# SSD's group norm taken out of its scan and applied in a pass beside the GLA scan

## The chip, the cores and the metric

The kernel runs on one core of a Trainium2 chip. The metric is the device time in microseconds of one execution of the whole program. A core has a matrix engine (TensorE, PE in the profile, with its weight loads as PEld), a vector engine (VectorE, DVE), a scalar engine (ScalarE, ACT), GpSimd (POOL) and a queue for transfers (SyncE, SP). Each engine works through its own list of instructions in order; semaphores make it wait for others. SBUF is the on-chip memory, PSUM the small memory of eight banks into which PE writes; POOL does not touch PSUM in this kernel.

## The reference

One decoder block on x (1024 tokens x 1024 channels, fp32): norm, one wide projection, two sequence mixers side by side (SSD, a Mamba-2 scan; GLA, gated linear attention), a gated merge, cross-attention to 256 memory tokens, a SwiGLU FFN and a last norm. The change concerns the end of the SSD mixer:

```python
def ssd_mixer(z, xBC, dt_raw, conv_w, conv_b, dt_bias, A_log, D_skip, norm_g):
    ...
    Lmat = segsum_exp(a)
    CB = jnp.einsum('bclgn,bcsgn->bcgls', Cc, Bc)
    y_diag = jnp.einsum('bcgls,bgrcls,bcsgrp->bclgrp', CB, Lmat, X)
    ...
    y_off = jnp.einsum('bclgn,bcgrpn,bgrcl->bclgrp', Cc, prev, jnp.exp(a_cs))
    y = (y_diag + y_off).reshape(Bsz, S, SSD_HEADS, P) + D_skip.astype(jnp.float32)[:, None] * x_heads
    y = y.reshape(Bsz, S, SSD_D_INNER) * jax.nn.silu(z.astype(jnp.float32))
    y = rmsnorm(y.reshape(Bsz, S, G, SSD_D_INNER // G), norm_g.reshape(G, SSD_D_INNER // G))
    return y.reshape(Bsz, S, SSD_D_INNER).astype(z.dtype)
```

So y is gated by silu(z), and then, for each token and each of two groups of 512 channels, divided by the root of the mean of its squares (plus EPS = 1e-6) and multiplied by a weight for each channel. The mixer's result is then multiplied by w_up_ssd.

## The kernel before, in words

**Layout and stages.** Activations lie transposed, 128 channels on the partitions and tokens along the row. The big products (w_in, the merge, the FFN) are split in fp32r halves: a weight block goes through ACT (whi, the rounded part, L224) and DVE (wlo, the rest), into a ring of three buffers each (wring, L227), and each block of a product takes three matmuls (high by high, high by low, low by high). Each 256-column unit of w_in runs as seven such products, named B11, T2, T1, B21, T3, B22 and T4 (class Unit, L276), which PE accumulates in banks acc; the sums of weight blocks that these need (sa, raw) are made on POOL or DVE, whichever two running meters (class Meter, `either`) put earlier. A unit's weights (raw, 1 MB) are loaded one unit ahead (L290), and results go to DRAM through SP (L469).

**What sets the order.** The framework records the instructions in program order with priorities and places each engine's list by its own model of time. `run(main, (side, rate), prio=PRIO)` (L439) takes one step of a generator beside every 1/rate steps of the main one and gives it a higher priority. Scans run in this way beside units of w_in.

**SSD's scan** (class SSD, L864) runs beside the units for r, q, k and one of gs, in 16 steps: 8 chunks of 128 tokens by 2 groups. `load` fetches x (xz, first half), B and C (bc), a broadcast row block (csb) and silu(z) (xz, second half) through SP. `lay` makes CB on PE into one PSUM bank, B's transpose into the same bank (copied out as bt by ACT, L893), and multiplies CB by the mask triu on DVE into the SBUF tile cbm. `decay` makes the decay e on ACT, and DVE multiplies e (128x1024) by cbm. `scan` makes y (bank py) and the new state. `gate` adds D times x (four DVE instructions), multiplies by silu(z) on POOL (128x512) and makes the sum of squares (sq on ACT, two sums on DVE, rd). `stat` sums over partitions with a small PE product (ones by rd) and forms rs by DVE and a POOL power. `norm` spreads rs along the row: DVE scales the identity by rs into diag, PE multiplies ones by diag (`spread`, L215), DVE multiplies y by the bank, and SP stores y to ys_d (L949). The calls are interleaved by `ssd_steps` (L951): scan, then stat of the step before with lay of the next, then gate, then norm of the step before with decay of the next. All small products take one of four PSUM banks called bank.

**GLA's scan** (class GLA, L997) runs beside three units of gs and three of gg in 43 steps over 8 chunks (`gla_steps`, L1074; run at L1108). Its tiles lie in a pool gl of their own.

**After it**, the last gg unit runs, and beside it `fetch` (L1203) loads ys_d block by block (128x1024) and splits it into high and low halves for the product by w_up_ssd; here it also applies ssd_norm, as a scale on ACT and as a scalar operand on DVE. All elementwise helpers record L73, all matmuls L51 and transposes L55, so a row of the profile is told apart by its tiles.

Of the kernel before, what the change touches and what calls it, by code (L numbers as in the profile page):

```python
# [78 lines left out]
def block_kernel(ctx: ExitStack, tc: tile.TileContext, t: dict, out: bass.AP):  # L79
# [39 lines left out]
    vm_d = dram("vm_d", MEM, D)  # L119
    cs_d = dram("cs_d", P, P)  # L120

    def acc():
# [37 lines left out]
    for a in range(2):  # L160
# [8 lines left out]
                       channel_multiplier=-1)  # L169
    mhalf = cp.tile([P, 8], F32, name="mhalf")  # L170
    POOL.memset(mhalf, -0.5)
# [550 lines left out]
    ebl = ep.tile([P, 4, NCH], F32, name="ebl")  # L722
    ewl = ep.tile([P, 4, NCH], F32, name="ewl")

    def conv(u, unit):
# [138 lines left out]
    class SSD:  # L864
# [8 lines left out]
        def load(s):  # L873
            g, tk = s.g, s.tk
            s.L = sp_.tile([P, 8, CH], F32, name="xz", tag="xz", bufs=3)
            SP.dma_start(s.L[:, 0:4], xbc_d[g * 512:(g + 1) * 512, tk].rearrange("(k p) s -> p k s", p=P))
            s.BC = sp_.tile([P, 2, CH], F32, name="bc", tag="bc", bufs=2)
            for i in range(2):
                r0 = 1024 + i * 256 + g * P
                SP.dma_start(s.BC[:, i], xbc_d[r0:r0 + P, tk])  # L880
            s.csb = sp_.tile([P, GH, CH], F32, name="csb", tag="csb", bufs=2)
            SP.dma_start(s.csb.rearrange("p h s -> p (h s)"),
                         cs_d[s.i0:s.i0 + GH, :].rearrange("h s -> (h s)").partition_broadcast(P))
            SP.dma_start(s.L[:, 4:8], sz_d[g * 512:(g + 1) * 512, tk].rearrange("(k p) s -> p k s", p=P))

        def lay(s):
            p = bank()
            PE.matmul(p[:, :P], s.BC[:, 0], s.BC[:, 1], start=True, stop=True)
            PE.transpose(p[:, P:2 * P], s.BC[:, 0], ident)
            s.cbm = sp_.tile([P, CH], F32, name="cbm", tag="cbm", bufs=2)  # L890
            mul(DVE, s.cbm, p[:, :P], triu)
            s.bt = sp_.tile([P, P], F32, name="bt", tag="bt", bufs=2)
            ACT.activation(s.bt, p[:, P:2 * P], AF.Copy)  # L893
            p = bank()
            for k in range(4):
                PE.transpose(p[:, k * P:(k + 1) * P], s.L[:, k], ident)
            s.xd = sp_.tile([P, GH, 64], F32, name="xd", tag="xd", bufs=2)
            mul(DVE, s.xd, p.rearrange("p (h d) -> p h d", d=64), s.heads(dt_h, 64))

        def decay(s):  # L900
            s.e = sp_.tile([P, GH, CH], F32, name="e", tag="e", bufs=2)
            for h in range(GH):
                ACT.activation(s.e[:, h], s.csb[:, h], AF.Relu, bias=cs[:, s.i0 + h:s.i0 + h + 1], scale=-1.0)
            ACT.activation(s.e, s.e, AF.Exp, scale=-1.0)
            ACT.activation(s.csb, s.csb, AF.Exp)
            s.xc = sp_.tile([P, GH, 64], F32, name="xc", tag="xc", bufs=1)
            mul(POOL, s.xc, s.xd, s.heads(dec, 64))
            mul(DVE, s.csb, s.csb, s.BC[:, 1].unsqueeze(1).to_broadcast([P, GH, CH]))
            mul(DVE, s.e, s.e, s.cbm.unsqueeze(1).to_broadcast([P, GH, CH]))

# [16 lines left out]
        def gate(s):  # L927
            s.y = sp_.tile([P, 4, CH], F32, name="y", tag="y", bufs=3)
            for k in range(4):
                DVE.scalar_tensor_tensor(s.y[:, k], s.L[:, k], dcol[:, s.g * 4 + k:s.g * 4 + k + 1],  # L930
                                         s.py[:, k * P:(k + 1) * P], ALU.mult, ALU.add)
            mul(POOL, s.y, s.y, s.L[:, 4:8])
            sq = sp_.tile([P, 4, CH], F32, name="sq", tag="sq", bufs=1)
# [5 lines left out]
        def stat(s):  # L939
            p = bank()  # L940
            PE.matmul(p[:, :1], s.rd, ones[:, :1], start=True, stop=True)
            s.rs = sp_.tile([P, 1], F32, name="rs", tag="rs", bufs=2)
            rsqrt(s.rs, p[:, :1], 1.0 / 512)

        def norm(s):
            p = bank()
            spread(p, s.rs, 1)
            mul(DVE, s.y, s.y, p[:, :P].unsqueeze(1).to_broadcast([P, 4, CH]))
            SP.dma_start(ys_d[s.g * 512:(s.g + 1) * 512, s.tk].rearrange("(k p) s -> p k s", p=P), s.y)  # L949

    def ssd_steps():  # L951
# [7 lines left out]
        for i in range(len(it) + 1):  # L959
# [15 lines left out]
            yield  # L975
            if z:
                z.norm()
            if b:
# [127 lines left out]

    gla = gla_steps()
    run(singles(gs[1:] + gg[:3], B, gg[3:]), (gla, 8 * 5 / 36), prio=PRIO)  # L1108
    drain(gla)
    st4.close()  # L1110
    st_early.close()
# [90 lines left out]

    def fetch(src, dst, gain=None):  # L1203

        for k in range(NB):
            x = hl(dst, k)
            raw = x[:, 1].bitcast(F32)
            SP.dma_start(raw, src[k * P:(k + 1) * P, :])
            if gain:
                ACT.activation(x[:, 0], raw, AF.Copy, scale=col(gain, k))  # L1210
                DVE.scalar_tensor_tensor(x[:, 1], raw, col(gain, k), x[:, 0], ALU.mult, ALU.subtract)
            else:
                ACT.activation(x[:, 0], raw, AF.Copy)
                sub(DVE, x[:, 1], raw, x[:, 0])
            yield
# [13 lines left out]

    get_ys = fetch(ys_d, i_ys, "ssd_norm")  # L1230
    for n, _ in enumerate(group(gg[3:], B)):
# [452 lines left out]
```

## Time and profile before

| What | Value |
|---|---|
| median of 3 runs | 1980.92 us (1979.81 to 1985.29) |
| the profiled execution | 1982.29 us |
| its span, first to last instruction | 1980.6 us |
| granted TensorE clock | 0.995 |
| mean transfer rate | 156 GB/s |
| SSD's first cs_d load and its last store are issued at | 395.1 us, 645.5 us |
| the first ys_d block is fetched | 808.5 us |

The profile is of one execution. Its page gives the busy time of each engine, and views of the trace give groups of instructions by line and tile, waits (who waited for whom: us in total, times, longest), busy time by stretch, and instructions in order of time. Where instructions are listed in order, the first two columns are the start and the duration in us, and brackets hold the idle time before it and what ended that. Matmuls overlap, so their price in the stream is read from starts, not from durations. In a tile's view the durations stand as minimum, median and maximum in ns.

### The profile page before, as it was taken

What the parts mean: (1) busy time and instruction counts of PE and PEld (TensorE: products, weight loads), DVE (VectorE), ACT (ScalarE), POOL (GpSimd) and SP (SyncE); (2) the same over time, 40 slices, a digit from 0 to 9 for tenths busy, and PEclk for the clock granted to TensorE, in tenths of its full rate; (3) what the DMA queues carried; (4) which work ended last, traced back from release to release, by engine and by line L of the source; (5) the groups of instructions that cost most, each with busy time, mean ns of one, the idle gap of its engine ahead of it and who ended that gap; (6) DMA issues with size and microseconds to landing.
All of it is one profiled execution on the core that took longest, in us unless ns stands there. A gap on an engine that the chain in (4) does not pass through costs nothing.

```text
span 1980.6 us, 26287 instructions
## 1 busy us (share of the span) xinstructions
PE 1932.2 (98%) x9772; PEld 1617.0 (82%) x9772; DVE 1323.7 (67%) x1884; ACT 859.5 (43%) x1503; POOL 600.5 (30%) x443
## 2 busy tenths in 40 slices
PE   7999899999999999999999999999999999999998
PEld 6898688777877888878888888877888888878887
DVE  5866679978887655564545237577877777774566
ACT  7534745465552444543223126453333333353243
POOL 1012343455554122112433000027544444420002
PEclk9999999999999999999999999999999999999999
DMA  9433233366553644797784201442234224185463
GB/s 308 142 119 99 99 120 112 113 196 181 178 174 105 214 155 133 281 381 255 257 297 150 70 32 42 139 139 80 80 105 135 80 91 140 47 288 207 160 225 124
DMA packets 236003, 309.59 MB, mean 156 GB/s; under 512 B 16714, under 2 KB 156212, under 8 KB 235876
## 3 DMA queue, kind: packets, MB, share of 16 engines
q1 hardware_dynamic: 235876, 307.92, 46.0%
q8 instruction: 77, 1.26, 0.3%
q14 instruction: 50, 0.41, 0.1%
HBM read 211.07 MB, written 96.80 MB: 155 GB/s over the span
## 4 chain that ended last, share of the span: by engine, by line
PE 75%; DVE 10%; issue 4%; ACT 4%; DMA 3%; POOL 3%; SPq 1%; POOLq 0%; ACTq 0%; DVEq 0%
PE acc L51 65%; PE bank L51 9%; DVE wlo L73 2%; DVE cv L73 2%; DVE o L73 1%; PE bank L55 1%; DMA raw<-in_w_in_dram 1%; DMA xt<-in_x_dram 1%; POOL raw L73 1%; POOL sa L73 1%; DMA fr<-act_d 1%; DVE fs L73 1%; POOL o L73 1%; ACT whi L224 1%; POOL y L73 0%
## 5 line engine op out<-in xcount | busy, mean ns | idle before, releaser
L51 PE MATMUL acc<-hl,wd 128*128 128x512 f32 x1920 | 439.9, 390 | 1.0 <-DVE gates L73 0.6
L51 PEld LDWEIGHTS acc<-hl,wd 128*128 128x128 f32 x1920 | 359.7, 188 | 76.9 <-DVE gates L73 1.3
L73 DVE TENSOR_TENSOR wlo<-raw,whi 128x512 fp32r<-128x512 f32 x272 | 248.3, 917 | 77.8 <-ACT whi L224 77.5
L224 ACT ACTIVATE whi<-raw 128x512 fp32r<-128x512 f32 x272 | 169.7, 628 | 245.2 <-PE acc L51 206.5
L73 DVE TENSOR_TENSOR o<-acc,o 128x512 f32<-128x512 f32 (+1 forms) x256 | 172.8, 676 | 121.2 <-PE acc L51 108.5
L73 POOL TENSOR_TENSOR sa<-raw 128x512 f32<-128x512 f32 x47 | 76.2, 1622 | 305.9 <-DMA raw<-in_w_ffn_in_dram 224.6
L51 PE MATMUL acc<-fs 128*128 128x512 f32 (+1 forms) x792 | 156.0, 356 | 2.0 <-ACT o L1579 1.8
L51 PEld LDWEIGHTS acc<-fs 128*128 128x128 f32 x792 | 130.6, 189 | 23.0 <-ACT o L1579 2.3
L73 POOL TENSOR_TENSOR raw<-raw,sa 128x512 f32<-128x512 f32 x48 | 69.2, 1441 | 253.0 <-DVE wlo L73 242.1
L224 ACT ACTIVATE fs<-fr 128x1024 fp32r<-128x1024 f32 (+1 forms) x84 | 79.8, 984 | 113.1 <-PE acc L51 38.3
L73 DVE TENSOR_TENSOR fs<-fr,fs 128x1024 fp32r<-128x1024 f32 (+1 forms) x84 | 99.7, 1219 | 38.5 <-ACT fs L224 38.2
L224 ACT ACTIVATE whi<-sa 128x512 fp32r<-128x512 f32 x96 | 59.9, 626 | 111.8 <-PE acc L51 111.7
L73 DVE TENSOR_TENSOR wlo<-sa,whi 128x512 fp32r<-128x512 f32 x96 | 82.4, 860 | 18.3 <-ACT whi L224 16.8
L224 ACT ACTIVATE wd<-raw 128x1024 fp32r<-128x1024 f32 x40 | 42.1, 1058 | 105.5 <-PE acc L51 104.1
L73 POOL TENSOR_TENSOR raw<-raw 128x512 f32<-128x512 f32 x48 | 82.9, 1726 | 4.5 <-DVE sa L73 4.3
L73 DVE TENSOR_TENSOR wd<-raw,wd 128x1024 fp32r<-128x1024 f32 x40 | 52.9, 1328 | 46.4 <-ACT wd L224 46.1
L51 PE MATMUL acc<-T1h,whi 128*128 128x512 f32 x192 | 76.4, 398 | 2.8 <-ACT whi L224 2.8
L51 PE MATMUL acc<-B22h,wlo 128*128 128x512 f32 x192 | 76.6, 399 | 1.5 <-DVE wlo L73 1.5
L51 PE MATMUL acc<-B21h,whi 128*128 128x512 f32 x192 | 75.8, 395 | 1.6 <-ACT o L353 1.6
L51 PE MATMUL acc<-B22h,whi 128*128 128x512 f32 x192 | 76.2, 397 | 1.1 <-DVE o L73 1.1
L51 PE MATMUL acc<-T4h,whi 128*128 128x512 f32 x192 | 75.8, 395 | 1.5 <-DVE o L73 1.5
L51 PE MATMUL acc<-B11h,whi 128*128 128x512 f32 x192 | 75.8, 395 | 1.2 <-ACT whi L224 1.2
(384 smaller groups left out, 4688.8 us busy)
## 6 DMA issues: line engine op xcount, KB each, us to landing
raw<-in_w_in_dram SPq DMA_DIRECT2D x26, 1024.0 KB, 5.8
raw<-in_w_ffn_in_dram SPq DMA_DIRECT2D x22, 1024.0 KB, 6.6
act_d<-o SPq DMA_DIRECT2D x77, 256.0 KB, 2.1
fr<-act_d SPq DMA_DIRECT2D x35, 512.0 KB, 6.5
pre<-in_w_ffn_out_dram SPq DMA_DIRECT2D x11, 1024.0 KB, 6.4
fr<-down_d SPq DMA_DIRECT2D x20, 512.0 KB, 3.6
down_d<-pre SPq DMA_DIRECT2D x33, 256.0 KB, 3.4
raw<-in_w_xkv_dram SPq DMA_DIRECT2D x8, 1024.0 KB, 6.2
```

The costliest lines, as they stand in the source:

```text
L51: return s.e.matmul(o, x, y, **kw)
L55: return s.e.transpose(o, x, i)
L73: return f(*a, **kw)
L224: ACT.activation(hi, src, AF.Copy)
```

## The change

- `stat` no longer forms the power and there is no `norm`. It writes the mean square plus EPS into one column of a new tile ysum (128 x 16, one column for each group and chunk).
- `gate` stores y as gated to ys_d at once. The product by silu(z) moves from POOL to DVE.
- CB's mask product moves from `lay` to `decay` and is written to the third quarter of CB's own PSUM bank; e is multiplied from there. The tile cbm goes away, and the bank is held from `lay` to `decay`.
- B and C come in one transfer instead of two.
- A new generator `ssd_norm` runs beside GLA's scan at 0.55 steps for each main step: one POOL power on ysum, one PE transpose, a copy, a store of the 16 rows to the DRAM tile rs_d; then, for each group and half of the tokens, a broadcast load of 512 scales (rb), and for each of four channel blocks a load of 128x512 from ys_d, one DVE instruction (y times ssd_norm times rb) and a store back to the same place: 16 such steps.
- `fetch` no longer has the gain: ACT copies, DVE subtracts.
- mhalf, the tile of exponents, has 16 columns instead of 8.

```diff
--- before.py
+++ after.py
@@ -118,6 +118,7 @@
     kT_d = dram("kT_d", D, MEM)
     vm_d = dram("vm_d", MEM, D)
     cs_d = dram("cs_d", P, P)
+    rs_d = dram("rs_d", NH, P)
 
     def acc():
         return ps.tile([P, 512], F32, name="acc", tag="acc", bufs=4)
@@ -167,7 +168,7 @@
     POOL.memset(ones, 1.0)
     POOL.affine_select(out=triu, in_=ones, pattern=[[1, P]], compare_op=ALU.is_ge, fill=0.0, base=0,
                        channel_multiplier=-1)
-    mhalf = cp.tile([P, 8], F32, name="mhalf")
+    mhalf = cp.tile([P, NH], F32, name="mhalf")
     POOL.memset(mhalf, -0.5)
 
     gcol, at = {}, 0
@@ -721,6 +722,7 @@
     ebm = ep.tile([P, 4, NCH], F32, name="ebm")
     ebl = ep.tile([P, 4, NCH], F32, name="ebl")
     ewl = ep.tile([P, 4, NCH], F32, name="ewl")
+    ysum = ep.tile([P, NH], F32, name="ysum")
 
     def conv(u, unit):
         cv = cvp.tile([P, 2, TOK], F32, name="cv", tag="cv", bufs=2)
@@ -875,20 +877,16 @@
             s.L = sp_.tile([P, 8, CH], F32, name="xz", tag="xz", bufs=3)
             SP.dma_start(s.L[:, 0:4], xbc_d[g * 512:(g + 1) * 512, tk].rearrange("(k p) s -> p k s", p=P))
             s.BC = sp_.tile([P, 2, CH], F32, name="bc", tag="bc", bufs=2)
-            for i in range(2):
-                r0 = 1024 + i * 256 + g * P
-                SP.dma_start(s.BC[:, i], xbc_d[r0:r0 + P, tk])
+            SP.dma_start(s.BC, xbc_d[1024:1536, tk].rearrange("(i g p) s -> g p i s", g=2, p=P)[g])
             s.csb = sp_.tile([P, GH, CH], F32, name="csb", tag="csb", bufs=2)
             SP.dma_start(s.csb.rearrange("p h s -> p (h s)"),
                          cs_d[s.i0:s.i0 + GH, :].rearrange("h s -> (h s)").partition_broadcast(P))
             SP.dma_start(s.L[:, 4:8], sz_d[g * 512:(g + 1) * 512, tk].rearrange("(k p) s -> p k s", p=P))
 
         def lay(s):
-            p = bank()
+            p = s.p = bank()
             PE.matmul(p[:, :P], s.BC[:, 0], s.BC[:, 1], start=True, stop=True)
             PE.transpose(p[:, P:2 * P], s.BC[:, 0], ident)
-            s.cbm = sp_.tile([P, CH], F32, name="cbm", tag="cbm", bufs=2)
-            mul(DVE, s.cbm, p[:, :P], triu)
             s.bt = sp_.tile([P, P], F32, name="bt", tag="bt", bufs=2)
             ACT.activation(s.bt, p[:, P:2 * P], AF.Copy)
             p = bank()
@@ -906,7 +904,9 @@
             s.xc = sp_.tile([P, GH, 64], F32, name="xc", tag="xc", bufs=1)
             mul(POOL, s.xc, s.xd, s.heads(dec, 64))
             mul(DVE, s.csb, s.csb, s.BC[:, 1].unsqueeze(1).to_broadcast([P, GH, CH]))
-            mul(DVE, s.e, s.e, s.cbm.unsqueeze(1).to_broadcast([P, GH, CH]))
+            cbm = s.p[:, 2 * P:3 * P]
+            mul(DVE, cbm, s.p[:, :P], triu)
+            mul(DVE, s.e, s.e, cbm.unsqueeze(1).to_broadcast([P, GH, CH]))
 
         def scan(s):
             st = state[s.g]
@@ -929,7 +929,8 @@
             for k in range(4):
                 DVE.scalar_tensor_tensor(s.y[:, k], s.L[:, k], dcol[:, s.g * 4 + k:s.g * 4 + k + 1],
                                          s.py[:, k * P:(k + 1) * P], ALU.mult, ALU.add)
-            mul(POOL, s.y, s.y, s.L[:, 4:8])
+            mul(DVE, s.y, s.y, s.L[:, 4:8])
+            SP.dma_start(ys_d[s.g * 512:(s.g + 1) * 512, s.tk].rearrange("(k p) s -> p k s", p=P), s.y)
             sq = sp_.tile([P, 4, CH], F32, name="sq", tag="sq", bufs=1)
             ACT.activation(sq, s.y, AF.Square)
             s.rd = sp_.tile([P, CH], F32, name="rd", tag="rd", bufs=2)
@@ -939,14 +940,8 @@
         def stat(s):
             p = bank()
             PE.matmul(p[:, :1], s.rd, ones[:, :1], start=True, stop=True)
-            s.rs = sp_.tile([P, 1], F32, name="rs", tag="rs", bufs=2)
-            rsqrt(s.rs, p[:, :1], 1.0 / 512)
-
-        def norm(s):
-            p = bank()
-            spread(p, s.rs, 1)
-            mul(DVE, s.y, s.y, p[:, :P].unsqueeze(1).to_broadcast([P, 4, CH]))
-            SP.dma_start(ys_d[s.g * 512:(s.g + 1) * 512, s.tk].rearrange("(k p) s -> p k s", p=P), s.y)
+            at = s.g * NCH + s.c
+            DVE.tensor_scalar(ysum[:, at:at + 1], p[:, :1], 1.0 / 512, EPS, ALU.mult, ALU.add)
 
     def ssd_steps():
         it = [SSD(c, g) for c in range(NCH) for g in range(2)]
@@ -973,8 +968,6 @@
             if a:
                 a.gate()
             yield
-            if z:
-                z.norm()
             if b:
                 b.decay()
             yield
@@ -1104,9 +1097,31 @@
                 c.load()
             yield
 
-    gla = gla_steps()
-    run(singles(gs[1:] + gg[:3], B, gg[3:]), (gla, 8 * 5 / 36), prio=PRIO)
+    def ssd_norm():
+        POOL.tensor_tensor(ysum, ysum, mhalf, ALU.pow)
+        p = bank()
+        PE.transpose(p[:NH, :P], ysum, ident)
+        rt = gl.tile([NH, P], F32, name="rt", tag="rt")
+        DVE.tensor_copy(rt, p[:NH, :P])
+        SP.dma_start(rs_d, rt)
+        yield
+        for g in range(2):
+            for j in range(2):
+                rb = gl.tile([P, HALF], F32, name="rb", tag="rb")
+                c0 = g * NCH + 4 * j
+                SP.dma_start(rb, rs_d[c0:c0 + 4, :].rearrange("c s -> (c s)").partition_broadcast(P))
+                for k in range(4 * g, 4 * g + 4):
+                    y = gl.tile([P, HALF], F32, name="yn", tag="yn", bufs=2)
+                    rows = ys_d[k * P:(k + 1) * P, half(j)]
+                    SP.dma_start(y, rows)
+                    DVE.scalar_tensor_tensor(y, y, col("ssd_norm", k), rb, ALU.mult, ALU.mult)
+                    SP.dma_start(rows, y)
+                    yield
+
+    gla, late = gla_steps(), ssd_norm()
+    run(singles(gs[1:] + gg[:3], B, gg[3:]), (gla, 8 * 5 / 36), (late, 0.55), prio=PRIO)
     drain(gla)
+    drain(late)
     st4.close()
     st_early.close()
 
@@ -1200,18 +1215,14 @@
     EVEN, ODD = ("op",) * 8, ("op",) * 6 + ("aux",) * 2
     i_ys, i_yg, i_wo, i_xq, i_q, i_xo = (paired(x) for x in (EVEN, ODD, EVEN, ODD, EVEN, EVEN))
 
-    def fetch(src, dst, gain=None):
+    def fetch(src, dst):
 
         for k in range(NB):
             x = hl(dst, k)
             raw = x[:, 1].bitcast(F32)
             SP.dma_start(raw, src[k * P:(k + 1) * P, :])
-            if gain:
-                ACT.activation(x[:, 0], raw, AF.Copy, scale=col(gain, k))
-                DVE.scalar_tensor_tensor(x[:, 1], raw, col(gain, k), x[:, 0], ALU.mult, ALU.subtract)
-            else:
-                ACT.activation(x[:, 0], raw, AF.Copy)
-                sub(DVE, x[:, 1], raw, x[:, 0])
+            ACT.activation(x[:, 0], raw, AF.Copy)
+            sub(DVE, x[:, 1], raw, x[:, 0])
             yield
 
     def fetch_gated(src, gate_src, dst):
@@ -1227,7 +1238,7 @@
                 split(g, x[:, 0, half(j)], x[:, 1, half(j)])
                 yield
 
-    get_ys = fetch(ys_d, i_ys, "ssd_norm")
+    get_ys = fetch(ys_d, i_ys)
     for n, _ in enumerate(group(gg[3:], B)):
         if n == 0:
             left.load(1)
```

## The prediction

> **What bounds the kernel now.** I read the head of the page first, then the table of busy time by stretch, then who TensorE (PE) waits for in the stretch that is changed, then PE's instructions in order of time. The page says that PE holds the span:
>
> ```profile
> span 1980.6 us, 26287 instructions
> ...
> PE 1932.2 (98%) x9772; PEld 1617.0 (82%) x9772; DVE 1323.7 (67%) x1884; ACT 859.5 (43%) x1503; POOL 600.5 (30%) x443
> ```
>
> SSD's small products lie between 394 us (first loads) and 646 us (last store), GLA's up to 786 us, and at 808 us the first ys_d block is fetched. The columns are busy us of PE, PEld, DVE, ACT, POOL, then granted clock, DMA share and GB/s:
>
> ```profile
> 394.00:646.00 252.00, 246.38 (x1508) 198.92 (x1506) 203.87 (x334) 127.55 (x274) 128.51 (x101) 1.00 0.54 167
> 646.00:786.00 140.00, 139.70 (x695) 118.71 (x694) 84.42 (x178) 66.05 (x162) 32.08 (x26) 1.00 0.55 172
> ```
>
> In the first stretch PE lacks 252 - 246.38 = 5.62 us, and VectorE (DVE) is the next engine, 81% busy. In the second PE lacks only 0.30 us and DVE is at 60%. So a microsecond is won in two ways only: PE instructions that go away, and PE waits that go away, nearly all of them in the first stretch. These are PE's waits there, then those from 646 to 830 us:
>
> ```profile
> PE bank L51 <- DVE diag L73: 2.7, 5, 0.9
> PE bank L51 <- DVE y L73: 1.1, 1, 1.1
> PE acc L51 <- DVE wlo L73: 1.0, 2, 0.5
> PE acc L51 <- ACT whi L224: 0.6, 1, 0.6
> PE acc L51 <- DVE o L73: 0.2, 1, 0.2
> ```
>
> ```profile
> PE bank L55 <- ACT o L1061: 0.3, 1, 0.3
> ```
>
> The first two of the five rows, 3.8 of 5.6 us, belong to the norm that the change takes out of the scan.
>
> **What goes on PE.** Sixteen norms each spread a row with one fp32 product, ones by diag, which PE runs as two instructions. Its price is read from the starts, since the durations overlap. First an undisturbed pair, then one that waits:
>
> ```profile
> 458.90 0.40 PE L51 MATMUL acc<-B11h,whi 128*128 128x512 f32 x1
> 459.14 0.39 PE L51 MATMUL bank<-diag,ones 128*128 128x128 f32 x2
> 459.28 0.47 PE L51 MATMUL acc<-B11l,whi 128*128 128x512 f32 x1
> 459.59 0.40 PE L51 MATMUL acc<-B11h,wlo 128*128 128x512 f32 x1
> ```
>
> ```profile
> 509.93 0.40 PE L51 MATMUL acc<-B22h,wlo 128*128 128x512 f32 x1
> 511.26 0.49 PE L51 MATMUL bank<-diag,ones 128*128 128x128 f32 x2 [0.93 <-DVE diag L73]
> ```
>
> Big matmuls start every 0.23 us (458.90 to 459.14). From the pair's start to that of the second matmul behind it are 0.45 us (459.14 to 459.59), so a pair costs 0.45 - 0.23 = 0.22 us, and 16 cost **3.5 us**. The waiting pair was due at 509.93 + 0.23 = 510.16 and started at 511.26: 1.10 us late, 0.17 more than the 0.93 that is booked as a wait. With that refill the five waits are 2.7 + 5 x 0.17 = **3.6 us**. The wait for y has its cause in these two rows, DVE's and then PE's:
>
> ```profile
> 451.08 0.67 DVE L73 TENSOR_TENSOR y<-y,bank 128x512 f32<-128x512 f32 x1
> ```
>
> ```profile
> 451.81 0.38 PE L51 MATMUL bank<-bc 128*128 128x128 f32 x1 [1.05 <-DVE y L73]
> ```
>
> The norm's product ends at 451.75, and PE's next small product, which wanted that PSUM bank, starts at 451.81. Norm's bank is gone after the change, so **1.1 us** more. In exchange CB's bank is held from lay to decay. That is before the next scan, which needs e anyway, so I charge nothing; if the cover failed, it would be one such wait of 1.1 us again.
>
> The other three rows (1.8 us) hang on how crowded DVE and ScalarE (ACT) are. DVE's and POOL's own rows in the stretch:
>
> ```profile
> L73 DVE TENSOR_TENSOR wlo<-raw,whi 128x512 fp32r<-128x512 f32 x45 | 43.2, 963 | 7.4 <-ACT whi L224 7.3
> L73 DVE TENSOR_TENSOR e<-e,cbm 128x1024 f32<-128x1024 f32 x16 | 29.7, 1857 | 2.1 <-ACT e L904 1.6
> L73 DVE TENSOR_TENSOR y<-y,bank 128x512 f32<-128x512 f32 x16 | 10.8, 676 | 0.2 <-PE bank L51 0.2
> L73 DVE TENSOR_SCALAR diag<-ident,rs 128x128 f32<-128x128 f32 x16 | 7.8, 488 | 7.9 <-POOL rs L73 7.9
> L73 POOL TENSOR_TENSOR y<-y,xz 128x512 f32<-128x512 f32 x16 | 22.7, 1419 | 14.8 <-DVE rs L73 11.6 <-DVE y L73 3.2
> L73 POOL TENSOR_TENSOR rs<-rs,mhalf 128x1 f32<-128x1 f32 x16 | 16.7, 1044 | 2.9 <-DVE rs L73 2.9
> ```
>
> DVE loses 10.8 + 7.8 = 18.6 us and gains z's product, 16 times 128x512 with both inputs in SBUF. The same form with both inputs in SBUF is wlo, and e has a PSUM input after the change, so the spreads (min/median/max ns) matter:
>
> ```profile
> L73 DVE TENSOR_TENSOR e<-e,cbm x16: 1225/2060/2359, 406.3 to 600.5; 128x1024 f32<-128x1024 f32 x16
> L73 DVE TENSOR_TENSOR y<-y,bank x16: 671/676/686, 435.5 to 644.8; 128x512 f32<-128x512 f32 x16
> L73 DVE TENSOR_TENSOR wlo<-raw,whi x45: 674/692/1821, 403.4 to 645.3; 128x512 fp32r<-128x512 f32 x45
> ```
>
> z's product then costs 16 x 0.674 = 10.8 to 16 x 1.821 = 29.1 us; I take wlo's mean, 16 x 0.963 = 15.4. Where one input is in PSUM (y<-y,bank) the spread is nil, so e may fall to its minimum, 29.7 - 16 x 1.225 = 10.1 us less, or not at all; I take the 10.1, since y<-y,bank is the nearest row. DVE: -18.6 + 15.4 - 10.1 = -13 us of 204 (ends: -18 and +10). CB's mask product keeps its size. POOL loses 22.7 + 15/16 of 16.7, so 38 of 128 us. ACT stops waiting for the mask before it copies bt, since that copy now comes first. And SP holds its loads less long:
>
> ```profile
> ACT bt L893 <- DVE cbm L73: 51.0, 13, 5.6
> ```
>
> ```profile
> SPq L876 <- POOL y L73: 46.0, 13, 6.9
> SPq L949 <- DVE y L73: 43.9, 15, 14.0
> ```
>
> None of this is on PE's path by itself; it shortens PE's last 1.8 us of waits. Ends: 0 and 1.8. I take **0.6 us**, the ACT row alone.
>
> The Trainium skill, "SBUF — State Buffer", section "Who interferes with whom", says that a DVE instruction with two SBUF inputs contends with a GpSimd instruction that reads SBUF, and one with at most one SBUF input does not. The rows above agree for wlo (up to 1821 ns) and y<-y,bank (at most 686 ns). By this rule e always takes its minimum (-10.1 us), while z's product can be held up (rival 1).
>
> **What is added.** At the head of the late pass PE makes one transpose, 0.27 us busy at most; I take 0.1 in its stream. It waits for a POOL power of 128x16: between 0 and 1.5 us, by the page's group rs with 1.04 us a piece at one column. I take **0.5** with the transpose inside. The late pass itself puts 16 DVE products (128x512, both inputs in SBUF: 16 x 0.69 = 11 us by the qk row's 692 ns below) and 37 transfers (1 + 4 + 16 + 16, 9.4 MB) beside GLA. DVE has 140 - 84 = 56 us free there; 9.4 MB in 140 us is 67 GB/s on top of 172, which scales the DMA share of 0.55 to 0.76. The danger is order, not load: a product whose load is late blocks DVE for the weight splits behind it, and SP's stores wait for the product with weight loads behind them. Bounds from the rows: DVE's wait for GLA's own loads, the landing times, and the ring of split weights:
>
> ```profile
> L73 DVE SCALAR_TENSOR_TENSOR qk<-qk,e 128x512 f32<-128x512 f32 x8 | 5.5, 692 | 15.8 <-DMA qk<-q_d 12.1 <-ACT e L1017 3.7
> ```
>
> ```profile
> bd<-bd_d SPq DMA_DIRECT2D x8, 256.0 KB, 5.1
> ```
>
> ```profile
> 691.68 0.68 DVE L73 TENSOR_TENSOR wlo<-raw,whi 128x512 fp32r<-128x512 f32 x1
> 698.57 0.40 PE L51 MATMUL acc<-B22h,whi 128*128 128x512 f32 x1
> ```
>
> This weight block is split by 692.36 and used at 698.57: 6.2 us of cover. DVE already waits 12.1 us for q_d in this stretch, and PE only 0.3 for anything. SP is covered too:
>
> ```profile
> 685.78 0.39 SPq L290 DMA_DIRECT2D raw<-in_w_in_dram  x1
> 709.28 0.48 PE L51 MATMUL acc<-B11h,whi 128*128 128x512 f32 x1
> ```
>
> A unit's weights are asked for 23.5 us before its first matmul, and a late store's hold is a landing plus a product, some 5.1 + 0.7 us. So I charge **0.5 us** (0 to 13.6, rival 2). The merged B and C loads (16 issues fewer) and the plain fetch of ys_d change no PE instruction; PE has no wait behind the fetch up to 830 us: nothing. If its cover went, the fetch could cost one block's landing.
>
> **Sum.** -3.5 - 3.6 - 1.1 - 0.6 + 0.5 + 0.5 = -7.8 us. The profiled execution took 1982.29 us (span 1980.6 and 1.7 around it), so it would be 1974.5; the median before is 1980.92, 1.4 lower, so I predict **1973.1 us**.
>
> **Rivals.**
> 1. *DVE takes PE's place in the scan.* For: DVE is 81% busy there, and z's product now stands in its order ahead of the square, the sums and the splits. If z's product takes 1.82 each and e gains nothing, DVE does 10 us more, and where it runs without a gap PE's waits return as waits for wlo. Then only the pairs' 3.5 us stay won and the added 1.0 is paid: 1978.4. Against: POOL, beside whose work such products stretch, has 38 of its 128 us less. The rule of the Trainium skill quoted above would hold z's product up so, but not e. Chance 0.17.
> 2. *The late pass blocks DVE* (slower). It decides where a load lands more than 6.2 us after its product's turn on DVE. The largest landing near by is that of the ys_d fetch after 808 us (512 KB each):
>
> ```profile
> L1208 SPq DMA_DIRECT2D hl<-ys_d x8: 319/320/531, 808.5 to 825.9; - x8
> ...
> DMA to landing us min/median/max: 9.6/9.6/9.6
> ```
>
> A block of that length costs PE 9.6 - 6.2 = 3.4 us; if four of the 16 fall so, 13.6 us: 1980.9 - 7.8 + 13.6 = 1986.7. For: every product has its own load just ahead, with two buffers. Against: GLA's loads of the same 256 KB land in 5.1 us, and no q_d wait cost PE anything. Chance 0.13.
> 3. *The relief is worth more.* All of the 5.6 us of waits go with their refills, ACT and POOL run ahead, and the added part costs nothing: -3.5 - 5.6 - 10 x 0.17 (ten booked waits) = -10.8, so 1970.1, and somewhat below. Chance 0.10.
>
> **How the numbers follow.** The forecast has 0.60, spread over 1970.5 to 1976.5 by the ends of its terms (refills, 1.8 us of other waits, 1.5 for the transpose). Time faster by over 0.3%, about what a measurement of this kernel can tell from no change, means under 1975.0: three quarters of the forecast (0.45) and rival 3 (0.10), so **0.55**. Within 0.3%: the rest of the forecast (0.15), rival 1 (0.17) and a part of rival 2 (0.03), so **0.35**. Slower: **0.10**. The range goes down past rival 3 and up past rival 1 to the start of rival 2's: **1968.5 to 1981.5**, which leaves out rival 2's larger part and the tail below.
>
> **What would show it.** PE instructions on diag fall by 32 in the scan, and no wait for diag or for y by bank is left there; DVE's e reads a PSUM input at 1.2 us with a small spread; POOL loses y and 15 powers. From 646 to 786 us PE's waits stay under 1 us though DVE waits for ys_d loads. I am wrong if PE waits for wlo in the scan by over 3 us, if it waits for wlo or o beside the late products, or if the instructions of PE are arranged anew and stages that the change doesn't touch move.

## The result, and the profile after

The changed kernel takes 1986.66 us (median, 1981.88 to 1998.41); the kernel before, in runs beside it, 1981.05. The ratio is 1.0031, with a 95% interval of 1.0021 to 1.0042: slower by 0.3%, or 5.6 us, where 1973.1 was forecast. Its profiled execution took 1985.88 us. The head of the page of the kernel after, and PE's line:

```profile
span 1983.9 us, 26230 instructions
...
PE 1924.4 (97%) x9741; PEld 1617.1 (82%) x9741; DVE 1321.0 (67%) x1885; ACT 861.1 (43%) x1503; POOL 563.6 (28%) x412
```

PE is busy 8 us less than before and the span is 3.3 us longer, so more PE waits were added than work went away. Busy time by stretch of the kernel after says where. SSD's last products on PE now run some ten microseconds sooner, so the border is put at 636 us instead of 646 (columns as in the prediction):

```profile
394.00:636.00 242.00, 238.69 (x1479) 197.37 (x1478) 188.15 (x330) 130.73 (x278) 89.02 (x69) 0.99 0.60 186
636.00:786.00 150.00, 137.29 (x669) 115.86 (x669) 93.03 (x181) 63.21 (x156) 31.90 (x25) 0.95 0.62 198
```

In the scan PE lacks 3.31 us (5.62 before), DVE and POOL have less to do, as forecast. Beside GLA PE lacks 12.71 us where it lacked 0.30, and its granted clock over the stretch is 0.95 where it was 1.00. Who PE waits for, first in the scan of the kernel after, then beside GLA and up to 800 us:

```profile
PE acc L51 <- ACT whi L225: 2.4, 1, 2.4
PE acc L51 <- DVE wlo L73: 0.9, 1, 0.9
```

```profile
PE bank L55 <- ACT o L1054: 5.2, 1, 5.2
PE acc L51 <- DVE o L73: 5.0, 1, 5.0
...
```

No wait for diag or for norm's bank is left in the scan. Beside GLA there are two waits of 5 us. The first, and an instruction of ACT ahead of it (start, duration, instruction, in brackets the wait):

```profile
675.96 0.47 PE L55 MATMUL bank<-ident,o 128*128 128x128 f32 x1 [5.20 <-ACT o L1054]
```

```profile
669.75 0.63 ACT L1010 ACTIVATE e<-bd 128x512 f32<-128x512 f32 x1 [6.94 <-DVE qk L73]
```

GLA's q product on DVE waited for q_d until 669.03. ACT's next exponential e has a single buffer, which that product frees, and waited for it for 6.94 us. The squares of o stand behind e in ACT's list, so they started only at 670.29, and the scaled o (L1054) that PE transposes came in time for 675.96. So ACT's list, too, hands a late q_d on to PE. The second wait, in PE's order of time:

```profile
714.75 0.39 PE L51 MATMUL acc<-B11l,whi 128*128 128x512 f32 x1
720.17 0.79 PE L51 MATMUL acc<-T4h,whi 128*128 128x512 f32 x1 [5.03 <-DVE o L73]
720.76 0.63 PE L51 MATMUL acc<-T4l,whi 128*128 128x512 f32 x1
721.19 0.63 PE L51 MATMUL acc<-T4h,wlo 128*128 128x512 f32 x1
...
724.17 0.41 PE L51 MATMUL acc<-T4h,whi 128*128 128x512 f32 x1
724.43 0.40 PE L51 MATMUL acc<-T4l,whi 128*128 128x512 f32 x1
```

The wait isn't its whole price. Behind it the big matmuls start 0.43 us apart (720.76 to 721.19) until 724.17, then 0.23 to 0.26 again: from 720.17 to 724.17 nine of them are issued in 4.00 us, for which full speed needs 2.07, so 1.9 us more. The Trainium skill, "TensorE: Matmul & The Clock Gate", section "HAM oscillation — how this bites in real kernels", describes this for a wait that crosses the gate's window: PE restarts at half its clock. The trace agrees here: the granted clock is 0.50 from 718 to 724 us and 1.00 again from 726.

Why was o late the second time? DVE of the kernel after, in order of time before that wait ended:

```profile
711.37 0.75 DVE L73 SCALAR_TENSOR_TENSOR yn<-yn,cols,rb 128x512 f32<-128x512 f32 x1 [1.40 <-DMA yn<-ys_d]
713.98 0.69 DVE L73 SCALAR_TENSOR_TENSOR qk<-qk,e 128x512 f32<-128x512 f32 x1 [1.86 <-DMA qk<-q_d]
...
716.07 0.75 DVE L73 SCALAR_TENSOR_TENSOR yn<-yn,cols,rb 128x512 f32<-128x512 f32 x1 [0.62 <-DMA yn<-ys_d]
...
719.43 0.68 DVE L73 TENSOR_TENSOR o<-acc,o 128x512 f32<-128x512 f32 x1
```

The product o<-acc, which frees the PSUM bank that PE wants at 714.98, stands in DVE's list behind two late products that wait for their loads and behind GLA's q product that waits for q_d. No single wait is over 2 us. The three are 3.9 us together, and with the two late products themselves (0.75 us each) they put off the products on S and the sums, which stand ahead of o in the same in-order list. And q_d is late because of SP's list. SP of the kernel after, ahead of the first of the two waits:

```profile
649.47 0.32 SPq L1006 DMA_DIRECT2D v<-v_d  x1
653.51 0.94 SPq L1116 DMA_DIRECT2D yn<-ys_d  x2
657.76 0.98 SPq L1118 DMA_DIRECT2D ys_d<-yn  x2
...
660.16 0.43 SPq L1065 DMA_DIRECT2D yg_d<-qk  x1
...
665.22 0.32 SPq L1118 DMA_DIRECT2D ys_d<-yn  x1
665.81 0.37 SPq L999 DMA_DIRECT2D qk<-q_d  x1
```

GLA's own transfers (v_d, yg_d, q_d) stand behind late loads and stores (L1116, L1118), most of which wait at the head of the list for a landing or a product. SP's three largest groups of waits on the late pass from 636 to 786 us in the kernel after (us in total, times, longest) come to 35.3 us:

```profile
SPq L1116 <- DMA ys_d<-yn: 19.9, 10, 4.9
...
SPq L1118 <- DVE yn L73: 9.0, 10, 2.0
...
SPq L1118 <- DMA yn<-ys_d: 6.4, 4, 3.0
```

### The profile page after: what moved, and what is told of

It reads as the page before. It is cut to its first block, busy times and chain, and to the rows that moved or that the text cites. A ratio compares the mean times of both kernels' runs of the same rounds, so it can differ in the third digit from the quotient of the medians.

```text
span 1983.9 us, 26230 instructions
## 1 busy us (share of the span) xinstructions
PE 1924.4 (97%) x9741; PEld 1617.1 (82%) x9741; DVE 1321.0 (67%) x1885; ACT 861.1 (43%) x1503; POOL 563.6 (28%) x412
## 4 chain that ended last, share of the span: by engine, by line
PE 76%; DVE 9%; DMA 5%; ACT 4%; issue 3%; POOL 2%; SPq 1%; POOLq 0%; ACTq 0%; DVEq 0%
PE acc L51 66%; PE bank L51 9%; DVE wlo L73 2%; DVE cv L73 2%; DVE o L73 1%; PE bank L55 1%; DMA xt<-in_x_dram 1%; DMA ys_d<-yn 1%; DMA fr<-act_d 1%; DMA yn<-ys_d 1%; DVE fs L73 1%; POOL o L73 1%; ACT whi L225 1%; DMA yg_d<-qk 1%; DMA raw<-in_w_in_dram 0%
## 5 line engine op out<-in xcount | busy, mean ns | idle before, releaser
L51 PE MATMUL acc<-T3h,whi 128*128 128x512 f32 x192 | 75.0, 391 | 2.4 <-ACT whi L225 2.4
```

Source lines behind the costliest of these rows:

```text
L51: return s.e.matmul(o, x, y, **kw)
```

## The experiments

Theory A: the late pass delays GLA's own chain (yg_d store, q_d load, q's product, squares, scale, transposes) by what stands ahead of it in the in-order lists of SP and DVE (and so of ACT), and PE pays with stalls and half a clock behind them. Rivals: the scan gained less than it seems; bytes; the ring of q/k tiles; the products as such; the order in which PE's list was arranged. Ratios are against the kernel before on the same chip, with 95% intervals; 0.001 is 2.0 us.

**The scan alone.** `run(singles(...), (gla, 8 * 5 / 36), prio=PRIO)` without `(late, 0.55)` and without `drain(late)`.

> The changed kernel without the late pass (y stays as gated, so the scale and the weights are left out). In the two traces PE's big matmuls run 10.7 us ahead of before at the end of SSD's scan and fall back 14.1 us beside GLA's. Theory: the late pass alone loses these 14 us, so this kernel keeps the scan's gain: 1970.5 us (1968 to 1973), and PE has no wait over 2 us between 636 and 786 us. Rival, the order: GLA's scan starts some 10 us earlier and is placed differently, and that makes the waits: 1983 to 1987 us, with waits of about 5 us still there.

1969.9 us, 0.9948 (0.9933 to 0.9962): 10.3 us are gained by the scan, and the whole late pass costs 0.0083, that is 16.4 us. Its stretch beside GLA, then three transfers of its SP list in order of time:

```profile
636.00:786.00 150.00, 150.00 (x745) 128.20 (x745) 85.48 (x175) 71.14 (x175) 36.25 (x28) 1.00 0.45 145
```

```profile
645.49 0.33 SPq L1006 DMA_DIRECT2D v<-v_d  x1
653.43 0.36 SPq L1065 DMA_DIRECT2D yg_d<-qk  x1
656.62 0.36 SPq L999 DMA_DIRECT2D qk<-q_d  x1
```

PE lacks nothing, and q_d is asked for 9.2 us sooner than in the changed kernel.

**The norm taken out of the kernel before.** `spread(p, s.rs, 1)` and the product by it are cut out of `norm` in the kernel before.

> The kernel before with the norm's spread and product left out of the scan (y is stored as gated after the same steps; scale left out, z's product on POOL and the mask in SBUF as before). This is the prediction's sum for what goes on PE by itself: 16 pairs at 0.22 us, their waits and the wait for norm's bank, 8.2 us: 1972 to 1974 us. Rival, the scan's 11 us come from the moves around it as well: 1976 us or more.

1972.41 us, 0.9952 (0.9937 to 0.9966), so 9.5 us with 6.7 to 12.5 as ends. The sum of the prediction's three PE terms for it, 3.5 + 3.6 + 1.1 = 8.2, lies inside; the run doesn't tell the three apart.

**Two parts of the scan undone**, each without the late pass: `mul(POOL, s.y, ...)` for z's product, and CB's mask in a tile cbm in SBUF as before.

> The scan's part of the change (no late pass; scale and weights left out) with z's product back on POOL. Theory of the prediction: DVE gets 12 us freer and POOL 22 us fuller, and neither is PE's bound there: within 2 us of the scan change alone, 1968 to 1972 us. Rival, part of the scan's gain came from z's move: 1973 us or more.

> The scan's part of the change (no late pass; scale and weights left out) with CB's mask product back in lay and its result in SBUF. Theory: e then stretches beside POOL again (1.2 us to over 1.5 us a piece on average) and ACT waits for the mask before bt, but PE has cover for both: within 2 us of the scan change alone (1969.9), 1968 to 1972 us. Rival, the scan's gain beyond the PE terms of the prediction comes from here: 1973 us or more.

1971.63 us, 0.9954 (0.9938 to 0.9970), and 1970.98 us, 0.9943 (0.9927 to 0.9960). Neither differs from the scan alone by what can be measured: what DVE and POOL save there did not shorten PE's time.

**The late pass taken apart.** Transfers without the product:

```diff
-                    DVE.scalar_tensor_tensor(y, y, col("ssd_norm", k), rb, ALU.mult, ALU.mult)
```

> The late pass keeps its 37 transfers but not its DVE products (ys_d is loaded and stored back as it is; the scale and the weights are left out). Theory, products that wait for their loads at the head of DVE's list: without products DVE never waits for ys_d, so 1971 to 1974 us. Rival, SP: late loads and stores hold SP's list, GLA's loads come late and PE waits all the same: 1980 us or more, with the DVE wait for q_d at 9 us or above as in the changed kernel.

And 16 products on a tile that stays in SBUF, without any transfer of the pass:

> The late pass keeps 16 DVE products of the same size, on a tile that stays in SBUF, without loads and stores (the scale and the weights are left out). Theory, waits for the loads: 1971 to 1974 us, and PE's waits beside GLA under 2 us. Rival, DVE's load: 16 x 0.75 = 12 us more work for DVE is what PE pays for: 1980 us or more.

Transfers alone: 1977.85 us, 0.9990 (0.9981 to 1.0000), so 8.3 us more than the scan alone. Products alone: 1974.17 us, 0.9966 (0.9955 to 0.9977), 3.6 us more. Together they cost 4.5 us beyond their sum. So the products as such are not the main part. In the profile of the products alone PE has one wait beside GLA, 1.93 us for a GLA product (qk) on DVE, and a stretch at half clock behind it.

**Priority and an earlier load.** The full late pass with no raised priority (`prios=(PRIO, 0)`), then with each ys_d load issued one step ahead of its product.

> The whole changed kernel, but the late pass gets no priority over the main products (GLA's scan keeps it). In the changed kernel its 16 products run between 647 and 716 us, 4.4 us apart. Theory, waits of products for their loads: spread further apart the buffers are free earlier and fewer products wait; 1972 to 1979 us. Rival, the order of GLA's scan: nothing changes there, 1983 us or more.

> The whole changed kernel, with each ys_d load issued one step of the late pass before its product (same two buffers, same transfers). Theory after the first runs: GLA's own transfers (q_d loads, yg_d stores) go round more slowly beside the late ones, and late products add their own waits on top. With the loads ahead the products' wait for ys_d (16.8 us over 9 waits in the changed kernel) falls under half, which saves the part that the two together cost above each alone, some 4 us: 1980 to 1984 us. Rival, the products' waits are all of it: 1974 us or less.

1982.77 us, 1.0010 (1.0000 to 1.0020): 4.2 us less than the changed kernel. So the order that priority gives the lists matters. 1988.3 us, 1.0029 (1.0016 to 1.0042): nothing. But the second edit did not do what it was to do: with two buffers the load ahead still waits for a store to land, and the products' waits for ys_d stayed at 16.2 us (16.8 in the changed kernel), where they were to fall under half. This run decides nothing about late loads.

**Bytes, and the ring of tiles.** Transfers alone with a quarter of the columns (`y[:, :P]`, `rows[:, :P]`), then the same with four q/k tiles in place of three.

> The kernel with the late transfers alone (no products; scale and weights left out), but each of the 36 moves 128 of its 512 columns: the same number of issues and waits on SP, a quarter of the bytes. The run with whole transfers took 7.9 us more than the scan change alone (1977.85 against 1969.9). Theory, bytes: GLA's transfers share the DMA engines with them, so three quarters of the loss go: 1970 to 1973 us. Rival, order: SP's list and the landing time of each store hold GLA's loads whatever their size: 1975 to 1979 us.

> The kernel with quarter-size late transfers (no products; scale and weights left out; 1976.9 us), with four buffers instead of three for GLA's q and k. Theory, the ring: a q_d load waits until the yg_d store of three chunks before has landed, DVE waits for that load, and each late transfer ahead of either on SP lengthens the trip; with a fourth buffer the load goes out a chunk earlier, DVE's wait for q_d falls under 8 us (19.7 before) and 3 us or more come back: 1970 to 1974 us. Rival, the late transfers cost PE in another way: 1975 us or more.

1976.86 us, 0.9980 (0.9969 to 0.9992), and 1977.82 us, 0.9981 (0.9971 to 0.9990). A quarter of the bytes costs 6.3 us more than the scan alone, where all of them cost 8.3, and with the fourth tile DVE's wait for q_d, which was to fall under 8 us, is 22.5 us (19.7 before). Neither bytes nor the ring is the main part for the transfers alone.

**What it is in SP's list.** The quarter transfers with ten buffers, loads five steps ahead of their stores, so that none of them waits at the head of the list:

```diff
-                    y = gl.tile([P, HALF], F32, name="yn", tag="yn", bufs=2)
+                ys.append((gl.tile([P, P], F32, name="yn", tag="yn", bufs=10), rows))
+                SP.dma_start(*ys[n])
+            if n >= 5:
+                SP.dma_start(*ys[n - 5][::-1])
```

> The late pass's transfers alone, with a quarter of the bytes, as in the run with quarter transfers (16 loads, 16 stores, 4 loads of scales, no products: the scale and the weights are left out), but arranged so that SP never has to wait at the head of its list for one of them: ten yn buffers of 128 columns, each store issued five steps after its load, each load into a buffer whose store went five steps before, and rs_d's store and the loads of the scales two and more steps after what they wait for. The number and the size of the late transfers stay. Theory A (the cost of the transfers is SP's in-order list: GLA's q_d load and yg_d store stand behind late transfers that wait a round trip each): 1969.5 to 1973 us, near the scan alone (1969.9), GLA's q_d loads again about 18 us apart, and no PE wait over 2 us between 640 and 790. Theory B (the number of transfers or their traffic slows GLA's own ones, whatever SP's list does): 1975 to 1979 us as with the quarter transfers (1976.9), with the q_d wait of 4 us or more and a PE stall behind L1054 or o again.

1977.41 us, 0.9981 (0.9971 to 0.9992). Theory A in this form missed. The waits at the head of SP's list that the late pass makes fall to 2.1 us (636 to 786 us in this kernel), and the loss stayed:

```profile
SPq L1111 <- DVE rt L73: 0.8, 1, 0.8
...
SPq L1115 <- DMA rb<-rs_d: 0.7, 2, 0.4
...
SPq L1120 <- DMA qk<-q_d: 0.3, 1, 0.3
SPq L1122 <- DMA qk<-k_d: 0.3, 1, 0.3
```

Its SP list in order of time shows why:

```profile
652.40 0.38 SPq L1006 DMA_DIRECT2D v<-v_d  x1
...
653.30 2.47 SPq L1122 DMA_DIRECT2D ys_d<-yn  x5
655.82 2.50 SPq L470 DMA_DIRECT2D gs_d<-o  x4
658.74 0.38 SPq L291 DMA_DIRECT2D raw<-in_w_in_dram  x1
659.24 0.61 SPq L1065 DMA_DIRECT2D yg_d<-qk  x1
...
667.21 0.36 SPq L999 DMA_DIRECT2D qk<-q_d  x1
```

Without waits the raised priority packs the late transfers into one block up to 655.8 us, at up to 0.49 us each (2.47 for 5), with w_in's stores and its 1 MB load pushed behind them and just ahead of GLA's yg_d store. That store is issued 5.8 us later than in the scan alone, and q_d, which waits until it has landed, follows after 8.0 us where it was 3.2: 10.6 us later in all. Two kernels tell this from the order of PE's list, which all three share but for ten lines: the same without raised priority, and the same bytes as 4 loads and 4 stores of four blocks.

> As the run with quarter transfers and no hold (36 late transfers of 64 KB and less, no products; scale and weights left out), but the late pass's steps get no raised priority. PE's, DVE's and POOL's lists keep their order (8 lines differ on DVE); on SP the stores of w_in and its 1 MB load of weights no longer stand right ahead of GLA's yg_d store, while the late transfers stay in one block ahead of it. Theory A (what stands in SP's list ahead of GLA's transfers decides): about half of the loss goes, 1972 to 1975 us, q_d's load follows the yg_d store by under 5 us. Theory B (the extra traffic, or the order of PE's list, which both kernels share): as with no hold, 1976 to 1979 us.

> As the run with quarter transfers and no hold, with the same bytes in a quarter of the transfers: 4 loads and 4 stores of four blocks of 128 columns each, 1 load of scales, 1 store of rs_d (no products; scale and weights left out). PE's list keeps the order of that run (10 lines differ). Theory A (SP's list: each late transfer takes its turn of about 0.45 us ahead of GLA's v_d, yg_d and q_d transfers): 1969.5 to 1973 us, near the scan alone (1969.9), GLA's first yg_d store again at about 654 us. Theory B (PE's planned order, in which the first transposes of o stand 23 big matmuls behind out's matmuls instead of 27, or the traffic): 1975 to 1979 us, with a PE wait of some 5 us between 665 and 695.

1972.9 us, 0.9965 (0.9952 to 0.9978), and 1970.23 us, 0.9948 (0.9933 to 0.9962). The first has the yg_d store as late, but q_d follows it after 3.4 us, and half of the loss is gone; the second kernel is back at the scan alone. The same three transfers in the second's SP list:

```profile
647.21 0.46 SPq L1006 DMA_DIRECT2D v<-v_d  x1
...
654.37 0.36 SPq L1065 DMA_DIRECT2D yg_d<-qk  x1
657.55 0.36 SPq L999 DMA_DIRECT2D qk<-q_d  x1
```

PE's only wait from 636 to 786 us goes the same way in the three profiles: 5.2 us for o with raised priority, 2.2 without, none with four blocks. So at a quarter of the bytes the cost of the transfers is what stands ahead of GLA's in SP's list: their number and the order that priority gives. Neither the bytes nor PE's arrangement is it, since the three share them but for three loads of scales. It isn't the waits at the head of the list either: the kernel with four blocks has 5.3 us of them on the late pass, more than the one that loses. Then with 16 DVE products of 128x512 on the loaded tiles:

> As the run with four blocks in each transfer (a quarter of the bytes in 4 loads and 4 stores), with 16 DVE products of 128x512 on the loaded tiles again, four for each load, with the identity in place of weights and scale (so scale and weights are left out): the number of DVE instructions and elements of the full late pass, without its many transfers. Theory A (the late pass costs by its transfers' turns on SP, and products cost only where they wait for loads and stores wait for them): 1970 to 1972.5 us. Theory B (the 16 products by themselves delay GLA's chain on DVE, as the run with products alone at 1974.2 suggests): 1974 to 1977 us, with a PE wait for DVE qk, o or L1054 and half a clock behind it.

1970.0 us, 0.9941 (0.9927 to 0.9954): the products cost nothing that can be measured where few transfers go with them.

**The full pass in larger transfers**: 8 loads and 8 stores of four blocks of 256 columns, one buffer of 4 KB (there is no room for two), with raised priority and without.

> The full late pass, nothing left out, in fewer and larger transfers: 8 loads and 8 stores of four blocks of 256 columns (512 KB each) and 8 loads of scales where the kernel has 16, 16 and 4; 32 DVE instructions of 128x256 for the 16 of 128x512; one yn buffer, so every load still waits for the store before it. Theory A (the number of turns and waits in SP's list sets the cost): 25 entries for 37, but each load and store still a round trip of some 8 us at the head of the list now and then: between the scan alone and the changed kernel, 1974 to 1980 us. Theory B (full bytes in use at the same time as GLA's own loads cost as much as the small ones): 1983 us and more.

> As the full late pass with four blocks in each transfer, without the raised priority for the late pass. Theory A: 1 to 4 us below that run (1972 to 1978 us), as with the low priority before. Theory B: the same as that run.

1987.66 us, 1.0033 (1.0020 to 1.0046), and 1989.86 us, 1.0039 (1.0025 to 1.0053): no better than the change, by either. I had expected 1974 to 1980; the rival, that the full bytes cost as much as the small transfers, had asked for 1983 and more, and it is the one that fits. SP's three largest groups of waits on the late pass in the first of the two, 636 to 800 us, add up to 36.7 us:

```profile
SPq L1131 <- DMA yn<-ys_d: 18.4, 6, 4.0
...
SPq L1116 <- DMA ys_d<-yn: 9.5, 6, 5.1
SPq L1131 <- DVE yn L73: 8.8, 5, 2.0
```

That is as much as in the changed kernel (35.3), against 5.3 in the kernel with four blocks of a quarter of the bytes. So fewer entries alone don't help the full pass. Whether these waits or the bytes themselves are its cost is not shown: full bytes with buffers enough were not tried, since there is no room for them.

**The scale put elsewhere.** The late pass is dropped behind its head, and `fetch` applies scale and weights, first through two half blocks on DVE, then with the product by the scale alternately on DVE and POOL and the weights inside the split, as before:

```diff
+            raw = x[:, 1].bitcast(F32)
+            SP.dma_start(raw, src[k * P:(k + 1) * P, :])
+            for j in range(2):
+                g = rp.tile([P, HALF], F32, name="ga", tag="ga")
+                mul((DVE, POOL)[j], g, raw[:, half(j)], rb[:, k // 4, half(j)])
+                ACT.activation(x[:, 0, half(j)], g, AF.Copy, scale=col("ssd_norm", k))
+                DVE.scalar_tensor_tensor(x[:, 1, half(j)], g, col("ssd_norm", k), x[:, 0, half(j)], ALU.mult, ALU.subtract)
```

> The changed kernel with the scale and the weights applied in the fetch of ys_d instead of in a late pass (16 DVE products of 128x512 and two broadcast loads for each group there; the 32 transfers of 256 KB beside GLA's scan are gone, the power, the transpose and the store of the scales stay). Theory, the late transfers beside GLA are the loss: the scan's gain stays, and the fetch has 4 us or less to pay, 1969 to 1974 us. Rival, the fetch is itself close to PE's need: PE waits there for hl, 1976 us or more.

> The changed scan with the scale in the fetch, as in the run that took 1980.7 us and lost 9 us to PE's waits for hl, but ys_d is loaded in whole blocks into its own place at once, both groups' scales come first, and the 16 products are shared by DVE and POOL, the weights going into the split as before the change. If the loads behind late buffers were that loss: 1970 to 1975 us, faster than both. If the added step between load and split is the loss wherever it stands: 1978 us or more.

1980.71 us, 1.0001 (0.9991 to 1.0011), with PE waits of 5.8 us in all at the fetch (three, the longest 3.3). The second: 1972.34 us, 0.9956 (0.9941 to 0.9970). It computes everything and beats both kernels, by 8.7 us against before. Its stretch beside GLA, and PE's only waits at the fetch (800 to 850 us):

```profile
636.00:786.00 150.00, 150.00 (x753) 128.39 (x752) 87.52 (x177) 70.51 (x175) 37.84 (x30) 1.00 0.45 145
```

```profile
PE acc L51 <- DVE hl L73: 1.5, 3, 0.6
```

## Why the prediction was wrong

- *Pairs, their waits, norm's bank (-8.2 us):* right as a sum; the run without the norm gives -9.5 (-6.7 to -12.5).
- *e at its minimum and z's product at 0.963 us:* right in kind. The tiles' rows of the kernel after:

```profile
L73 DVE TENSOR_TENSOR e<-e,bank x16: 1206/1210/1222, 410.7 to 606.5; 128x1024 f32<-128x1024 f32 x16
```

```profile
L73 DVE TENSOR_TENSOR y<-y,xz x16: 677/692/1570, 419.9 to 621.1; 128x512 f32<-128x512 f32 x16
```

  e has no spread left with one input in PSUM, and z's product mostly takes 0.69 (mean 0.744, 11.9 us in all), so DVE is relieved by 18.6 - 11.9 + 10.3 = 17 us where 13 was taken. Rival 1's condition, z's product at 1.82 each and no gain on e, did not arise. Undone, neither edit moved the time.
- *The scan as a whole (-8.8):* the run of the scan alone gives -10.3, near rival 3.
- *POOL's power at the head (bounds 0 and 1.5 us):* the upper bound was too low for the power itself, which took twice as long, but PE didn't wait for it. The group of the kernel after:

```profile
L73 POOL TENSOR_TENSOR ysum<-ysum,mhalf 128x16 f32<-128x16 f32 x1 | 2.9, 2942 | 0.0
```

- *The late pass, "So I charge **0.5 us** (0 to 13.6, rival 2)":* this is the step that failed. It costs 16.4 us, above its own upper end, and it turns -10.3 into +6. Two sentences led there. "SP is covered too" was read from w_in's weights, asked for 23.5 us ahead; GLA's own yg_d store and q_d load have no such lead, and stand in the same list. "No q_d wait cost PE anything" was read at DVE's 12.1 us of waits, with no late product in DVE's list around q. And the prediction's own sign of being wrong, a PE wait for o beside the late products, came.
- *Rival 2* named the side and, with 1986.7 us, the size. Its mechanism was not what happened: it asked for a ys_d load more than 6.2 us behind its product's turn, four times. The kernel after has 4.2 us at the longest, and transfers without any product cost 8.3 us. At the second stall three waits under 2 us, two of them of late products, added up in DVE's list; that far it named the right place. The 1986.7 was met by luck.
- *"If the instructions of PE are arranged anew"* was named as a way to be wrong. They were: counted in PE's list, the transposes of o of GLA's second chunk stand 15 big matmuls behind out's own products, and 28 in the scan alone, so that wait has 13 x 0.23 = 3.0 us less cover. It is the first of the two stalls. How much of the 16.4 us this makes isn't settled: the runs with a quarter of the bytes keep 27 or more there, so they don't test it. A stall also comes without it: in the run of the transfers alone PE waits 5.2 us for a later chunk's o though 35 big matmuls stand ahead of that wait.

Settled, then: the scan won about what was forecast, and the late pass lost it beside GLA. For the transfers with a quarter of the bytes the cause is shown: their entries in SP's list ahead of GLA's. For the full pass the delays in in-order lists and the half clock behind the stalls are read from its trace, and no run takes them away one by one. Open stays how its 16.4 us divide between SP's list, the bytes, waiting products in DVE's list, and PE's new arrangement.

## What to carry to other kernels

A pass that is put beside another stage is priced by what it stands ahead of in each in-order list, the transfer queue first: follow the host stage's own store-to-load chain and ask how long it can be held, rather than how busy the engines are. With a quarter of the bytes, 8 late loads and stores cost nothing here; the same bytes in 36 transfers cost 6.5 us. The full bytes in few transfers and one buffer did cost, so that rule is not shown for them. A PE stall of several microseconds is to be priced with the half-clock stretch behind it, here 5.0 + 1.9 us.

## What the runs showed of the hardware

The clock also fell behind shorter waits than those of 5 us. In the run with products alone a wait of 1.93 us was followed by it; PE of that kernel in order of time:

```profile
634.97 0.40 PE L51 MATMUL acc<-B11l,whi 128*128 128x512 f32 x1
637.29 0.49 PE L51 MATMUL bank<-qk 128*128 128x128 f32 x2 [1.93 <-DVE qk L73]
...
640.08 0.63 PE L51 MATMUL acc<-T4l,whi 128*128 128x512 f32 x1
640.51 0.63 PE L51 MATMUL acc<-T4h,wlo 128*128 128x512 f32 x1
640.94 0.49 PE L51 MATMUL acc<-T4h,whi 128*128 128x512 f32 x1
641.26 0.39 PE L51 MATMUL acc<-T4l,whi 128*128 128x512 f32 x1
```

The matmuls start 0.43 us apart until 640.94, and the granted clock is 0.50 from 638 to 641 us. The Trainium skill, "TensorE: Matmul & The Clock Gate", section "Why this matters for your kernels", advises against PE gaps of over some 3 us; this one was shorter, 2.3 us from start to start. Length alone does not decide: in the same kernel a wait of 1.95 us for ACT's whi, ended at 410.09, left the granted clock at 1.00, and so did one of 2.20 us in the run without holds at low priority, while one of 2.12 us in the run with quarter transfers brought 0.50. In the scan of the kernel before, with waits of up to 1.1 us, it stayed at 1.00.
